# One 512-column product for both halves of the activations in the 256-token dense tiles

## Chip, core and metric

The kernel runs on one core of one Trainium2 chip. The metric is device time in microseconds for one launch: 3149.86 us is the median of three runs before the change (3148.79 to 3150.08). The engines are named as the profile names them: PE (TensorE matmul), PEld (TensorE weight load), DVE (VectorE), ACT (ScalarE), POOL (GpSimd) and SP (SyncE, which issues most DMAs).

## What is computed

Two model blocks in float32 on 256 tokens of width 2048: a gated recurrent mixer, an attention layer with shared keys and values, then a block of convolution and windowed attention, and a layer that looks up experts by product keys and uses all 16384 expert rows. What matters here are the dense products with 2048 rows. In the second block, for example:

```python
proj = xn @ w_in + b_in                       # 256 x 2048 by 2048 x 3328
x = x + mixed @ w_out
qh = (xt @ peer_w_q).reshape(T, PEER_HEADS, 2, PEER_HALF)
...
v1, i1 = lax.top_k(sub[:, :, 0], PEER_TOPK)   # top 16 of 128, per token, head and half
```

The first block's dense products cover 272 positions (16 fixed ones and the 256 tokens) or the 256 tokens alone.

## The kernel before

Every dense product is done with split operands. A weight tile of 128 x 128 is split by `split` (lines 191 to 193): ACT copies it to a rounded type (`wh`, line 192) and DVE subtracts to get the rest (`wl`, line 193). The activations are split the same way into a high and a low part, which lie side by side in one tile `x[128, 2, 16, 272]` (`new_xs`, line 205). A product is then three matmuls per block of 128 rows: wh by high, wl by high, wh by low, all into one accumulator of 128 x 256 or 128 x 272 (`Dense.products`, line 117, matmul at line 127). A job with 16 blocks has 48 such matmuls. PSUM holds two accumulators (`psacc`, two buffers), each in a bank of its own.

Jobs run in a list, in the order in which they are appended, under `run`. At the start of job n, `run` calls the read-out (`evac`) of job n-1, then issues the four quarters of job n's products. Ahead of the first quarter it issues the split of the second half of job n+1's weights, and ahead of the third the split of the first half of job n+2's. `wh` and `wl` have two buffers per half, so a split waits until the matmuls of two tiles before have read the buffer. After each quarter `run_side` issues a piece of side work (attention, convolution, top-16 searches) until a credit per job is used up (`BUDGET`). The order of all queues is thus fixed when the program is built, and each engine works through its queue in that order.

The stages that hold jobs of 256 tokens and 16 blocks, with the read-out of each, are:

- stage f (587 to 1036 us): attention projections. 32 of its 64 tiles have 256 columns (query and gate); DVE scales the accumulator into `pj` (line 763).
- f-out (1036 to 1132 us): 16 tiles; DVE adds the accumulator to `hT` (line 899).
- stage b (1132 to 1376 us): 26 tiles of the second block's input product; DVE scales into `qb` (lines 1416, 1518) or `gt` (line 1524). For the 10 tiles of line 1416 ACT then adds a bias.
- stage p (1498 to 1605 us): 16 tiles of `peer_w_q`; ACT alone copies the accumulator into `qh` (line 1891). The side work is `peer_head` and `peer_pairs`: for each head the top 16 of 128 on DVE (`top16`, lines 1731 to 1741) and the top 16 of the candidates.

Behind p comes a stretch (1605 to about 1860 us) in which the first 29 `UBlock` jobs multiply expert rows (line 1967) while the rest of the top-16 work and then the building of gate grids (`grid_gen`, lines 1998 to 2021) run beside them; the hook of the 30th block waits until the grids are issued in full (`v_hook`). From block 29 on, a `UBlock` already uses the other form of product: one matmul of wh with both activation halves, 512 columns (line 1958), and one of wl with the high half, 256 columns (line 1959), and a read-out in which ACT copies the second half (line 1977), DVE adds the first (line 1978), and ACT applies the activation function (line 1979). The rest, to 3148 us, alternates such blocks with `VPair` jobs (line 2111).

Of the kernel before, what the change touches and what calls it, by code (L numbers as in the profile page):

```python
# [8 lines left out]
F32 = mybir.dt.float32  # L9
# [6 lines left out]
AF = mybir.ActivationFunctionType  # L16
OP = mybir.AluOpType
# [4 lines left out]
KB = 16  # L22
NM = 16
S = 256
# [56 lines left out]
class Dense:  # L81
# [4 lines left out]
    def __init__(self, k, chunk, j, xs, ts, evac, hook=None, after=None):  # L86
        self.k, self.chunk, self.j, self.xs, self.ts = k, chunk, j, xs, ts
        self.evac_fn, self.hook, self.after = evac, hook, after
        self.w = [None, None]

    def load(self):
        while len(self.chunk.setdefault("raws", [])) * 8 < self.chunk["nk"]:
            self.load_part()
# [23 lines left out]
    def products(self, b0, b1, by_block=True):  # L117
        k, c = self.k, self.chunk
        xh, xl = self.xs()
        n = c["nk"] // 2  # L120
        blocks = [(b, t) for b in range(b0, b1) for t in range(3)]
        if not by_block:
            blocks.sort(key=lambda bt: (0, 2, 1)[bt[1]])
        for b, t in blocks:
            wh, wl = self.w[b // n]
            a, x = ((wh, xh), (wl, xh), (wh, xl))[t]
            k.PE.matmul(self.acc, a[:, b % n], x[:, c["k0"] + b, self.ts], start=(b == 0 and t == 0),  # L127
                        stop=(b == c["nk"] - 1 and t == 2))

    def open(self):  # L130
        self.acc = self.k.psacc.tile([128, self.ts.stop - self.ts.start], F32, name="acc")

    def mm(self):
        self.open()
# [1 line left out]
        return [lambda i=i: self.products(i * nk // 4, (i + 1) * nk // 4) for i in range(4)]  # L136

    def evac(self):
        self.evac_fn(self.acc)


class Kit:
# [3 lines left out]
def body(tc, x, meta, gamma_lb, a_norm, a_w_in, a_out_norm, a_w_out, kv_norm, kv_w, fox_b_f,  # L146
         fox_k_norm, b_norm, b_w_in, b_q_norm, b_w_out, positions, norm1_g, w_in, b_in, conv_w,
         conv_b, ln_g, ln_b, q_norm_g, k_norm_g, sinks, w_out, norm2_g, peer_w_q, sub_keys,
         peer_u, peer_v, cst, out, dbg=None):
    with tc.manual_schedule():  # L150
        _body(tc, x, meta, gamma_lb, a_norm, a_w_in, a_out_norm, a_w_out, kv_norm, kv_w, fox_b_f,
              fox_k_norm, b_norm, b_w_in, b_q_norm, b_w_out, positions, norm1_g, w_in, b_in, conv_w,
              conv_b, ln_g, ln_b, q_norm_g, k_norm_g, sinks, w_out, norm2_g, peer_w_q, sub_keys,
              peer_u, peer_v, cst, out, dbg)


def _body(tc, x, meta, gamma_lb, a_norm, a_w_in, a_out_norm, a_w_out, kv_norm, kv_w, fox_b_f,
# [4 lines left out]
    V, A, G, PE = nc.vector, nc.scalar, nc.gpsimd, nc.tensor  # L162
    K = Kit()
# [10 lines left out]
    early = tc.alloc_tile_pool(name="early", bufs=1)  # L174
    psacc = tc.alloc_tile_pool(name="psacc", bufs=2, space=PSUM, reuse_waits="tile")
    ps = tc.alloc_tile_pool(name="psA", bufs=1, space=PSUM, reuse_waits="tile")
    wk = tc.alloc_tile_pool(name="wkA", bufs=1, reuse_waits="tile")
# [18 lines left out]
    def split_g(h_blk, g, oh, ol):  # L196
        A.activation(oh, h_blk, AF.Copy, scale=g)
        V.scalar_tensor_tensor(ol, h_blk, g, oh.bitcast(F32), op0=OP.mult, op1=OP.subtract)

    def flat(t):  # L200
        return t.rearrange("p h t -> p (h t)")

    whole = {}

    def new_xs(pool, tag):
        x = pool.tile([128, 2, KB, T], F32R, name=tag)
        whole[tag] = x
        return x[:, 0], x[:, 1]

    def wview(w):  # L210
        return w.rearrange("(k p) c -> p k c", p=128)
# [13 lines left out]
    def rsqrt_steps(pool, ps_list, scale, out_t, tags, less=None):  # L225
        n = sum(math.prod(p.shape[1:]) for p in ps_list)
        v, r, t = (pool.tile([128, n], F32, name=g) for g in tags)
        srcs, c = [], 0
        for p in ps_list:
            m = math.prod(p.shape[1:])  # L230
            srcs.append((slice(c, c + m), p if len(p.shape) == 2 else flat(p)))
            c += m

        for c, src in srcs:
            V.tensor_scalar(v[:, c], src, scale, EPS, op0=OP.mult, op1=OP.add)
        if less is not None:
            V.tensor_tensor(v, v, less, op=OP.subtract)
        yield 0.1 + n / 960
        yield 1
        A.activation(r, v, AF.Ln)  # L240
        A.activation(r, r, AF.Exp, scale=-0.5)
        A.activation(t, r, AF.Square)
        yield 3
        V.scalar_tensor_tensor(t, t, -0.5, v, op0=OP.mult, op1=OP.mult)
        out_t = r if out_t is None else out_t
        V.scalar_tensor_tensor(out_t, t, 1.5, r, op0=OP.add, op1=OP.mult)
        yield 0.2 + n / 480
        return out_t
# [217 lines left out]
    for t in vtz:  # L466
        G.memset(t[:, 0], 0.0)

    xh, xl = new_xs(xs1, "xs")
    cur = {"x": (xh, xl)}  # L470
    tok = ((0, NM), (NM, 128), (NM + 128, 128))
    st = {}
# [24 lines left out]
    def start_sums(g):  # L497
        for i in (1, 2):
            n = tok[i][1]
            sq = wk.tile([128, 2, T], F32, name="sq", bufs=2)  # L500
            src = x_raw[i][:, g * 512:(g + 1) * 512]
            if i == 2:
                V.scalar_tensor_tensor(flat(sq)[:n, :512], src, 1.0, src, op0=OP.mult, op1=OP.mult,
                                       accum_out=ssp[:n, i, g:g + 1])
            else:
                A.activation(flat(sq)[:n, :512], src, AF.Square, accum_out=ssp[:n, i, g:g + 1])
            if g == 3:
                V.tensor_reduce(ss[:n, i:i + 1], ssp[:n, i], axis=AX.X, op=OP.add)
# [14 lines left out]
    def start_rest():  # L523
        p = ps.tile([128, 4, 128], F32, name="tp", bufs=3)
        PE.transpose(p[:, 0], pk2, ident)
        for i in range(2):
            PE.transpose(p[:, 1 + i, :124], pk3[:, i], ident[:124, :124])
        PE.transpose(p[:, 3], pk1, ident)
        V.tensor_copy(par[:, 128:], p[:, 0])
        V.tensor_copy(par[:, 16:128], p[:, 3, 16:])  # L530
        V.tensor_copy(taps.rearrange("p (a b) -> p a b", a=2), p[:, 1:3, :124])
        gm = wk.tile([128, KB], F32)
        g0 = par[:, P1["gamma"]:P1["gamma"] + KB]
        g1 = par[:, P1["gamma"] + KB:P1["gamma"] + 2 * KB]
        V.tensor_tensor(gm, g0, g1, op=OP.max)
        ge = wk.tile([128, 2, KB], F32)
        V.tensor_tensor(ge[:, 0], g0, gm, op=OP.subtract)
        V.tensor_tensor(ge[:, 1], g1, gm, op=OP.subtract)
        A.activation(ge, ge, AF.Exp)
        V.tensor_tensor(gm, ge[:, 0], ge[:, 1], op=OP.add)  # L540
        V.reciprocal(gm, gm)
        V.tensor_tensor(lbs[:, 0], ge[:, 0], gm, op=OP.mult)
        V.tensor_scalar(lbs[:, 1], lbs[:, 0], -0.5, 0.5, op0=OP.mult, op1=OP.add)
        V.tensor_tensor(lbs[:, 0], lbs[:, 0], lbs[:, 1], op=OP.add)
        st["o"] = new_xs(early, "ys")
# [205 lines left out]
    def chunk(wv, c0, k0=0, nk=KB):  # L751
        return {"wv": wv, "c0": c0, "k0": k0, "nk": nk}
# [157 lines left out]
    def a_out_hook():  # L910
        st["kv"] = new_xs(xs1, "xs")
# [279 lines left out]
    for i, (hp, u) in enumerate(order):  # L1191
        wv, c0, xs, ts, half, bufs = fspec[u]
# [335 lines left out]
    for t in "q0 c0 q1 c1 q2 c2 q3 c3".split():  # L1528
        n = int(t[1])
# [118 lines left out]
    for i, part in enumerate(PARTS):  # L1648
# [3 lines left out]
        k0, nk = (0, 8) if part == "c" else (8 + 2 * int(part[0]), 2 * len(part))  # L1652
        for c2 in range(KB // 2):
            c = chunk(wvo, c2 * 256, k0, nk)
            for j in range(2):
                jobs.append(Dense(K, c, j, lambda: st["mix"], xcols,
                                  lambda acc, n=c2 * 2 + j, f=on_tile: f(n, acc), hook if c2 + j == 0 else None))
# [225 lines left out]
    for h in range(8):  # L1883
        c = chunk(wvq, h * 256)
# [316 lines left out]
```

## Time and profile before

| | |
|---|---|
| runs before | 3149.86 us median, 3148.79 to 3150.08 |
| profiled execution | 3149.75 us, span 3147.9 us |
| mean granted TensorE clock | 0.992 |
| PE busy | 3068.7 us (97% of the span), 20863 matmuls |
| DVE busy | 2394.4 us (76%) |
| ACT busy | 1657.4 us (53%) |

The profiled execution lies 0.11 us under the median and 1.85 us over its own span. Shares of busy time are means over stages with different limits, so they are read stage by stage: the view of windows gives each engine's busy time in a stretch, the view of waits says who waited for whom, and the timeline gives the start of single instructions. The duration of a matmul in the profile covers its way through the array and overlaps the next; the pace is the distance from start to start.

### The profile page before, as it was taken

The numbers are of one execution on the slowest core, as the hardware profiler recorded it, in microseconds if no ns is written. First come the engines' busy times: TensorE is split into PE (matmuls) and PEld (weight loads), VectorE is DVE, ScalarE is ACT, GpSimd is POOL, SyncE is SP. The second block draws the span as 40 slices with busy tenths as digits, with TensorE's granted clock in tenths as the row PEclk, the third lists the DMA queues.
The fourth block names the chain that finished last, engine by engine and source line by source line (L and its number), as shares of the span: only waits on it lengthen the run. The fifth ranks groups of instructions, "written<-read, shape, count | busy, mean of one in ns | idle before, by whom it ended". The sixth has DMA issues, their size and how long they took to land.

```text
span 3147.9 us, 51907 instructions
## 1 busy us (share of the span) xinstructions
PE 3068.7 (97%) x20863; PEld 2834.8 (90%) x20863; DVE 2394.4 (76%) x3828; ACT 1657.4 (53%) x2640; POOL 250.9 (8%) x185
## 2 busy tenths in 40 slices
PE   8999999999999999988999989999999999999999
PEld 7999999999999999988998987888888888888887
DVE  6666666665666667768788988888888898989874
ACT  5455554566566556746543445544545454545443
POOL 1000000000000000000000003211112020303020
PEclk9999999999999999998999999999999999999999
DMA  6545445554544553324533777777777676767754
GB/s 208 155 138 157 138 134 161 160 157 140 161 148 148 173 172 111 109 89 140 183 136 123 211 219 204 202 205 205 204 196 210 189 220 185 214 189 226 196 192 161
DMA packets 362130, 540.64 MB, mean 172 GB/s; under 512 B 13771, under 2 KB 270128, under 8 KB 356112
## 3 DMA queue, kind: packets, MB, share of 16 engines
q1 hardware_dynamic: 325248, 501.33, 54.1%
q10 hardware_dynamic: 33200, 16.85, 1.9%
q0 software_dynamic: 3440, 19.13, 1.8%
q8 instruction: 164, 2.69, 0.4%
q14 instruction: 78, 0.64, 0.1%
HBM read 518.38 MB, written 18.87 MB: 171 GB/s over the span
## 4 chain that ended last, share of the span: by engine, by line
PE 85%; DVE 10%; ACT 3%; issue 1%; POOL 1%; DMA 1%; SPq 0%; DVEq 0%; ACTq 0%
PE acc L127 37%; PE y L2111 22%; PE acc L1958 11%; PE acc L1959 6%; DVE wl L193 3%; PE cv L1475 1%; DVE o L2001 1%; ACT wh L192 1%; PE acc L1967 1%; DVE o L1999 1%; DVE tb L2000 1%; DVE tb L1998 1%; PE o L1110 1%; DVE e L1814 0%; DVE qh L1932 0%
## 5 line engine op out<-in xcount | busy, mean ns | idle before, releaser
L193 DVE TENSOR_TENSOR wl<-raw,wh 128x1024 fp32r<-128x1024 f32 (+1 forms) x724 | 863.1, 1199 | 513.5 <-ACT wh L192 511.3
L192 ACT ACTIVATE wh<-raw 128x1024 fp32r<-128x1024 f32 (+1 forms) x724 | 728.8, 1016 | 466.1 <-PE acc L127 324.9
L127 PE MATMUL acc<-xs,wh 128*128 128x272 f32 (+1 forms) x4064 | 794.6, 292 | 21.1 <-ACT xs L192 11.4
L127 PEld LDWEIGHTS acc<-xs,wh 128*128 128x128 f32 x4064 | 648.0, 191 | 25.4 <-ACT xs L192 12.5
L127 PE MATMUL acc<-xs,wl 128*128 128x272 f32 (+1 forms) x2032 | 584.9, 288 | 0.0
L127 PE MATMUL acc<-ys,wh 128*128 128x256 f32 (+1 forms) x2880 | 555.2, 288 | 5.4 <-DVE qb L1416 3.1
L1958 PE MATMUL acc<-xs,wh 128*128 128x512 f32 x1584 | 556.3, 393 | 0.0
L127 PEld LDWEIGHTS acc<-ys,wh 128*128 128x128 f32 x2880 | 454.6, 189 | 9.2 <-ACT sinT L1255 3.3
L192 ACT ACTIVATE wh<-qh 128x512 fp32r<-128x512 f32 x396 | 250.7, 633 | 388.3 <-DVE qh L1932 359.4
L1959 PE MATMUL acc<-xs,wl 128*128 128x256 f32 x1584 | 443.8, 280 | 0.8 <-DVE wl L193 0.8
L127 PE MATMUL acc<-ys,wl 128*128 128x256 f32 (+1 forms) x1440 | 406.6, 282 | 0.0
L1932 DVE STREAM_TRANSPOSE qh<-raw 128x512 f32<-128x512 f32 x396 | 403.5, 1058 | 1.7 <-DMA raw<-in_peer_u_dram 1.7
L127 PEld LDWEIGHTS acc<-xs,wl 128*128 128x128 f32 x2032 | 386.8, 191 | 0.9
L1958 PEld LDWEIGHTS acc<-xs,wh 128*128 128x128 f32 x1584 | 297.6, 188 | 67.2
L2111 PE MATMUL y<-wh,ah 128*128 128x512 f32 x1024 | 317.9, 391 | 2.4 <-ACT wh L192 2.4
L2111 PE MATMUL y<-wl,ah 128*128 128x512 f32 x1024 | 317.1, 391 | 1.5 <-DVE wl L193 1.5
L2111 PE MATMUL y<-wh,al 128*128 128x512 f32 x1024 | 316.7, 390 | 0.0
L193 DVE TENSOR_TENSOR wl<-qh,wh 128x512 fp32r<-128x512 f32 x396 | 296.2, 756 | 19.3
L1959 PEld LDWEIGHTS acc<-xs,wl 128*128 128x128 f32 x1584 | 297.8, 188 | 5.0 <-DVE wl L193 1.6
L127 PEld LDWEIGHTS acc<-ys,wl 128*128 128x128 f32 x1440 | 272.5, 189 | 1.7
L2111 PEld LDWEIGHTS y<-wl,ah 128*128 128x128 f32 x1024 | 192.3, 188 | 43.3 <-DVE wl L193 2.3
L2111 PEld LDWEIGHTS y<-wh,al 128*128 128x128 f32 x1024 | 192.5, 188 | 42.0
(473 smaller groups left out, 3555.8 us busy)
## 6 DMA issues: line engine op xcount, KB each, us to landing
raw<-in_peer_v_dram SPq DMA_DIRECT2D x128, 1024.0 KB, 5.2
raw<-in_peer_u_dram SPq DMA_DIRECT2D x396, 256.0 KB, 5.1
raw<-in_a_w_in_dram SPq DMA_DIRECT2D x64, 1024.0 KB, 5.9
raw<-in_kv_w_dram SPq DMA_DIRECT2D x32, 1024.0 KB, 5.6
raw<-in_b_w_in_dram SPq DMA_DIRECT2D x32, 1024.0 KB, 5.3
raw<-in_peer_u_dram SPq DMA_DIRECT2D x29, 1024.0 KB, 4.9
raw<-in_w_in_dram SPq DMA_DIRECT2D x26, 1024.0 KB, 5.3
raw<-in_a_w_out_dram SPq DMA_DIRECT2D x16, 1024.0 KB, 5.4
```

The lines of the kernel that those rows point to most:

```text
L127: k.PE.matmul(self.acc, a[:, b % n], x[:, c["k0"] + b, self.ts], start=(b == 0 and t == 0), stop=(b == c["nk"] - 1 and t == 2))
L192: A.activation(dh, src, AF.Copy)
L193: V.tensor_tensor(dl, src, dh.bitcast(F32), op=OP.subtract)
L1110: PE.matmul(po[:, b * 128:(b + 1) * 128], vt[:, i], pts[:, 2 * b + i], start=(i == 0), stop=(i == nt - 1))
L1475: PE.matmul(acc, dgs[k0][:, k - k0], hp[:, k:k + S], start=(k == 0), stop=(k == n - 1))
L1932: V.transpose(ut[g].rearrange("p k (e s) -> p e k s", e=4), u[:, :, k:k + 4])
L1958: PE.matmul(self.acc, uh[:, k % 8], both[:, :, k, xcols], start=(k == 0), stop=False)
L1959: PE.matmul(self.acc[:, 0], ul[:, k % 8], nh[:, k, xcols], start=False, stop=(k == KB - 1))
L1967: PE.matmul(self.acc, a[:, k % 8], c[:, k, xcols], start=(k == 0 and t == 0), stop=(k == KB - 1 and t == 2))
L1998: V.tensor_tensor(e2, words, at(wd[:, 1], t0), op=OP.is_equal)
L1999: V.tensor_tensor(o2, e2, at(one, t0), op=OP.mult)
L2111: PE.matmul(self.y[tb][q], a[:, r, ts], c[:, q * 512:q * 512 + 512], start=(self.place == 0 and h == 0 and i == 0), stop=(self.place == GR ...
```

## The change

A job is wide if it has 16 blocks and 256 columns. Its accumulator becomes 128 x 2 x 256. For each block it issues one matmul of wh with both halves of the activations (512 columns) and one of wl with the high half (256 columns, into the first half of the accumulator). At the read-out `meet` is called first: ACT copies the second half of the accumulator to a tile in SBUF, DVE adds the first half in place, and the job's own read-out gets that tile instead of the accumulator. The tile is `hsq` (one buffer, shared with the sums of squares) up to the end of f-out, and `mt` (one buffer) in stages b and p. 90 tiles are wide: 32 in f, 16 in f-out, 26 in b, 16 in p. The tiles of 272 columns, the 32 tiles of 8 blocks between b and p, and the expert blocks are as before.

```diff
+        self.wide = chunk["nk"] == KB and ts.stop - ts.start == S
...
     def products(self, b0, b1, by_block=True):
         k, c = self.k, self.chunk
         xh, xl = self.xs()
         n = c["nk"] // 2
+        if self.wide:
+            both = k.whole[id(xh)]
+            for b in range(b0, b1):
+                wh, wl = self.w[b // n]
+                k.PE.matmul(self.acc, wh[:, b % n], both[:, :, c["k0"] + b, self.ts], start=(b == 0), stop=False)
+                k.PE.matmul(self.acc[:, 0], wl[:, b % n], xh[:, c["k0"] + b, self.ts], start=False, stop=(b == c["nk"] - 1))
+            return
...
     def open(self):
-        self.acc = self.k.psacc.tile([128, self.ts.stop - self.ts.start], F32, name="acc")
+        n = self.ts.stop - self.ts.start
+        self.acc = self.k.psacc.tile([128, 2, n] if self.wide else [128, n], F32, name="acc")
...
     def evac(self):
-        self.evac_fn(self.acc)
+        self.evac_fn(self.k.meet(self.acc) if self.wide else self.acc)
...
+    def meet(acc):
+
+        t = (wk if "hpad" in st else early).tile([128, S], F32, name="mt" if "hpad" in st else "hsq")
+        A.activation(t, acc[:, 1], AF.Copy)
+        V.tensor_tensor(t, t, acc[:, 0], op=OP.add)
+        return t
```

In the changed kernel lines from the middle of the file on stand 20 further down (line 193 is 202 there, line 1891 is 1911).

The first place is ACT's queue in stage p, at the end of one tile; before:

```order
L1891 ACTIVATE qh<-acc 128x256
L192 ACTIVATE wh_16760<-raw_16476 128x1024
L192 ACTIVATE wh_16794<-raw_16654 128x1024
L1755 ACTIVATE skT<-tp 128x256
L1891 ACTIVATE qh<-acc 128x256
L192 ACTIVATE wh_16844<-raw_16656 128x1024
```

and now:

```order
L212 ACTIVATE mt<-acc 128x256
L1911 ACTIVATE qh<-mt 128x256
L201 ACTIVATE wh_15720<-raw_15472 128x1024
L201 ACTIVATE wh_15746<-raw_15624 128x1024
L1775 ACTIVATE skT<-tp 128x256
L212 ACTIVATE mt<-acc 128x256
L1911 ACTIVATE qh<-mt 128x256
```

ACT's copy into `qh` now stands behind a first copy into `mt`, and reads a tile that DVE has to finish in between; the split of the next weights (`wh`) is still behind it.

The second place is DVE's queue in the same stage (L1731 to L1741 and, shifted, L1751 to L1761 are the top-16 search); before:

```order
L1731 MAX v_16219<-tb 128x8 x2
L1733 MAX_INDEX i_16924<-v_16219,tb 128x8 x2
L1736 MATCH_REPLACE tb<-v_16219,tb 128x128 x2
L1738 MAX v_16219<-tb 128x8 x2
L193 TENSOR_TENSOR wl_17016<-raw_16831,wh_17015 128x1024
L1741 MAX_INDEX i_16924<-v_16219,tb 128x8 x2
```

and now:

```order
L1751 MAX v_15257<-tb 128x8 x2
L1753 MAX_INDEX i_15855<-v_15257,tb 128x8 x2
L1756 MATCH_REPLACE tb<-v_15257,tb 128x128 x2
L1758 MAX v_15257<-tb 128x8 x2
L213 TENSOR_TENSOR mt<-mt,acc 128x256
L202 TENSOR_TENSOR wl_15937<-raw_15775,wh_15936 128x1024
L1761 MAX_INDEX i_15855<-v_15257,tb 128x8 x2
```

The new addition (`mt<-mt,acc`) stands straight ahead of the subtraction that makes `wl`, and behind the top-16 work of the tile before. Nothing else changes its place.

## Rows read from the trace of the kernel before

**Rows 1.** The page: busy time of each engine, and the chain that ended last, by engine.
```profile
PE 3068.7 (97%) x20863; PEld 2834.8 (90%) x20863; DVE 2394.4 (76%) x3828; ACT 1657.4 (53%) x2640; POOL 250.9 (8%) x185
...
PE 85%; DVE 10%; ACT 3%; issue 1%; POOL 1%; DMA 1%; SPq 0%; DVEq 0%; ACTq 0%
```

**Rows 2.** Windows by stage; columns: stretch, its length, busy us (instructions), PEclk, DMA, GB/s.
```profile
core 0: us, PE busy (x) PEld busy (x) DVE busy (x) ACT busy (x) POOL busy (x), PEclk, DMA share, GB/s
587.40:1036.00 448.60, 445.85 (x3565) 437.26 (x3563) 293.57 (x526) 276.16 (x437) 0.00 (x0) 1.00 0.50 151
1036.00:1131.80 95.80, 93.77 (x781) 93.57 (x779) 58.91 (x85) 46.75 (x70) 1.58 (x4) 0.98 0.56 176
1131.80:1376.40 244.60, 229.70 (x1691) 219.03 (x1690) 159.56 (x293) 152.58 (x325) 0.00 (x0) 0.97 0.36 113
...
1527.00:1605.20 78.20, 78.20 (x670) 78.20 (x669) 68.95 (x270) 38.48 (x64) 4.33 (x6) 1.00 0.54 172
1605.20:1732.00 126.80, 119.63 (x993) 116.76 (x993) 113.99 (x397) 52.69 (x97) 0.00 (x0) 1.00 0.35 125
1732.00:1859.00 127.00, 113.23 (x1190) 109.20 (x1190) 122.75 (x169) 61.27 (x116) 0.00 (x0) 1.00 0.73 216
```

**Rows 3.** Windows: eleven whole tiles of f-out (48 matmuls each), same columns.
```profile
1063.69:1126.17 62.48, 62.48 (x530) 62.48 (x529) 39.65 (x55) 31.11 (x44) 0.00 (x0) 1.00 0.61 194
```

**Rows 4.** Timeline of PE: one expert block, 32 matmuls, first and next job's first.
```profile
2007.13 0.40 PE L1958 MATMUL acc<-xs,wh 128*128 128x512 f32 x1
2007.36 0.28 PE L1959 MATMUL acc<-xs,wl 128*128 128x256 f32 x1
...
2012.70 0.40 PE L2111 MATMUL y<-wh,ah 128*128 128x512 f32 x1
```

**Rows 5.** ACT's read-outs by source line: ns least/median/most, first and last start.
```profile
L1891 ACT ACTIVATE qh<-acc x16: 367/386/388, 1507.7 to 1605.2; 128x256 f32<-128x256 f32 x16
...
L1977 ACT ACTIVATE ga<-acc x99: 357/384/387, 1892.3 to 3023.8; 128x256 f32<-128x256 f32 x99
```
**Rows 6.** The same for the addition in the expert blocks, and who waited for it.
```profile
L1978 DVE TENSOR_TENSOR ga<-ga,acc x99: 406/420/423, 1892.8 to 3024.3; 128x256 f32<-128x256 f32 x99
...
  ACT ga L1979: 78.5, 99
```

**Rows 7.** Timeline of PE: where f-out waits for a free accumulator; idle time in brackets.
```profile
1050.70 0.48 PE L127 MATMUL acc<-xs,wh 128*128 128x256 f32 x1 [2.03 <-DVE hT L899]
```

**Rows 8.** Timeline of ACT in stage p, over two tile ends.
```profile
1558.97 0.39 ACT L1891 ACTIVATE qh<-acc 128x256 f32<-128x256 f32 x1 [0.95 <-PE acc L127]
1559.25 1.05 ACT L192 ACTIVATE wh<-raw 128x1024 fp32r<-128x1024 f32 x1
1561.81 1.06 ACT L192 ACTIVATE wh<-raw 128x1024 fp32r<-128x1024 f32 x1 [1.50 <-PE acc L127]
1565.53 0.38 ACT L1891 ACTIVATE qh<-acc 128x256 f32<-128x256 f32 x1 [2.66 <-PE acc L127]
```

**Rows 9.** Timeline of DVE in the same stretch.
```profile
1557.05 1.21 DVE L193 TENSOR_TENSOR wl<-raw,wh 128x1024 fp32r<-128x1024 f32 x1
...
1559.61 0.48 DVE L1738 MAX8 v<-tb 128x8 f32<-128x128 f32 x2
1560.34 1.23 DVE L193 TENSOR_TENSOR wl<-raw,wh 128x1024 fp32r<-128x1024 f32 x1 [0.26 <-ACT wh L192]
```

**Rows 10.** Waits of DVE from 1527 to 1605.2 us: total us, times, longest.
```profile
DVE wl L193 <- ACT wh L192: 8.5, 13, 1.5
```

**Rows 11.** Timeline of DVE after stage p, three waits around the gates.
```profile
1713.36 0.69 DVE L193 TENSOR_TENSOR wl<-tp,wh 128x512 fp32r<-128x512 f32 x1 [1.49 <-ACT wh L192]
1716.79 0.69 DVE L193 TENSOR_TENSOR wl<-tp,wh 128x512 fp32r<-128x512 f32 x1 [0.47 <-ACT wh L192]
1718.73 0.69 DVE L193 TENSOR_TENSOR wl<-tp,wh 128x512 fp32r<-128x512 f32 x1 [1.25 <-ACT wh L192]
```

**Rows 12.** Waits of PE from 1732 to 1859 us.
```profile
PE g L2019 <- DVE o L2001: 13.6, 12, 2.8
```

More of the change, by code (lines that the diff above doesn't have):

```diff
@@ L198, in split_g @@
         V.scalar_tensor_tensor(ol, h_blk, g, oh.bitcast(F32), op0=OP.mult, op1=OP.subtract)
+    def meet(acc):
[3 more added lines that the diff above has]
+        return t
+    K.meet = meet
     def flat(t):
         return t.rearrange("p h t -> p (h t)")
-    whole = {}
+    K.whole = whole = {}
+    keep = []
     def new_xs(pool, tag):
         x = pool.tile([128, 2, KB, T], F32R, name=tag)
-        whole[tag] = x
-        return x[:, 0], x[:, 1]
+        h = x[:, 0]
+        whole[tag] = whole[id(h)] = x
+        keep.append(h)
+        return h, x[:, 1]
     def wview(w):
```

## The prediction

> **What bounds the kernel now.** I read the page first: PE is busy for 97% of the span, and 85% of the chain that ended last is PE's [rows 1]. So what PE no longer has to stream counts, unless another engine is the limit where it is saved. The view of windows by stage tells where that is so [rows 2]. In f and f-out PE is busy for all but 2.8 of 448.6 us and 2.0 of 95.8 us, while DVE and ACT are below two thirds. In b PE has 15 us without work, DVE and ACT are at 65% and 62%. In p it is another picture: PE is busy without a gap, but DVE is busy for 68.95 of 78.2 us, so it has only 9.25 us left, and 8.5 of these are spent waiting for `wh` [rows 10]. Behind p, from 1605 to 1859 us, DVE sets the pace: 122.75 of the last 127 us, and there it is PE that waits, 12 times, 13.6 us, for the operands `o` that DVE builds [rows 2, 12]. The reader should keep this in mind: p lies directly ahead of a stretch that runs at DVE's speed, and its DVE work is in the same queue.
>
> **What the change removes on PE.** The pace of the narrow form is read from eleven tiles of f-out without other work between them: 62.48 us, 5.680 us a tile, 118.3 ns a matmul [rows 3]. The wide form already runs in the expert blocks: the same 16 blocks, from the first matmul to the next job's first, 2007.13 to 2012.70, take 5.57 us [rows 4]. So a product of 512 columns costs nearly what two of 256 cost (0.23 and 0.12 us from start to start), and a wide tile saves only 0.11 us, 2%, although it has a third fewer matmuls. For 74 tiles in f, f-out and b that is 8.1 us; with the 16 of p 9.9 us. The granted clock is 1.00 in both rows, so no difference of clock is in this. Bounds: 0.09 to 0.12 us a tile, by the last digit of the timeline.
>
> The Trainium skill (TensorE: Matmul & The Clock Gate, section "Back-to-back issue gap") puts the distance of warm matmuls at N / 2.4 + 2.5 ns. By that a narrow tile would take 5.24 us and a wide one 5.20, and the 74 tiles would save 3.0 us instead of 8.1. The rows show 118.3 ns, not 109, so I keep to the rows.
>
> **What it adds at the read-out.** ACT's copy of the second half: 0.38 us; DVE's addition: 0.42 us [rows 5, 6]. Both exist in this trace in the same form, so these prices are not in doubt. What they cost is a matter of what stands behind them in each queue.
>
> In f, f-out and in the 16 gate and value tiles of b, ACT goes from its copy straight to the split of the next weights. DVE's addition and its own read-out (0.42 each) lie beside that `wh` copy of 1.05 us, for which DVE's next `wl` had to wait anyway. In the 10 tiles of b with a bias ACT already waited for DVE; there the chain gets 0.8 us longer. All of it is covered by two thirds use of both engines and by two accumulators, of which each has a whole tile (5.7 us) to come free. I take 0; if that cover were gone, each read-out would cost up to 0.8 us. One place has no cover: in f-out the third tile waits 2.03 us for an accumulator that a DVE addition frees [rows 7]; it now also waits for the copy, +0.4 us.
>
> **Stage p is different.** Here ACT's copy into `qh` reads what DVE has added, and the copy that makes `wh` is queued behind it; on DVE the addition stands directly ahead of the `wl` that needs this `wh`. So at each tile end DVE adds (0.42), ACT copies to `qh` (0.28 until its next instruction starts), ACT makes `wh` (1.06), and DVE has nothing else to do until then; with two hand-overs of 0.04 that is 1.8 us from the start of the addition to the start of `wl` [rows 6, 8, 9]. Before, DVE came from its top-16 search and found `wh` ready or nearly so: 0.26 us of waiting at 1560.34 [rows 9]. 12 of the 16 read-outs fall between 1527 and 1605.2 us. They add 12 x 1.8 = 21.6 us to DVE's queue; DVE's former idle time, 9.25 us, goes into that. The first three, where DVE has room, and the last one I put at 1.3 us together. DVE then ends stage p 13.6 us later than it would have.
>
> PE does not feel this at once. The `wl` made at 1560.34 to 1561.57 is needed only in the second half of the following tile, about 1565.53 + 2.84 = 1568.4, so there are 6.8 us of slack [rows 8, 9]. Beyond that PE waits for `wl`, its 1.8 us saved in p are gone, and DVE enters the next stretch late.
>
> **What is made up behind p.** From 1732 to 1859 us nothing can be: DVE has 4.25 us idle in 127, and PE waits for it [rows 2, 12]. From 1605 to 1732 us DVE is idle for 12.8 us. A wait behind `wh` is only saved if ACT waited for PE there, and most of these follow DVE's own results through ACT; I take the three around the gates, 1.49 + 0.47 + 1.25 = 3.2 us [rows 11]. The bounds are 0 and 12.8. After 1859 us PE is the limit again and everything is shifted as a whole.
>
> **The sum**, against the profiled execution of 3149.75 us: -8.1 (74 tiles) + 0.4 (f-out) + 13.6 (DVE's delay in p) - 3.2 (made up) = +2.7, so 3152.5 us. With the bounds of what is made up, 3142.9 to 3155.7. The median of the runs before is 0.11 us higher than this execution, which changes nothing. A measurement of this kernel can tell about 0.2%, 6.3 us, from no change.
>
> **Rivals.**
>
> 1. *DVE absorbs the read-outs of p.* 12 additions of 0.42 us are 5.0 us, less than the 9.25 idle, and PE has 6.8 us of slack at each tile. If the hand-over to ACT costs DVE no idle time, or the whole delay is made up before 1732 us, all 90 tiles save 0.11 us: 3149.75 - 9.9 + 0.4 = 3140.3 us. For it: PE waits for nothing in p now. Against it: the order of both queues, and 78.5 us in 99 cases, 0.79 us each, that ACT waits for the same addition in the expert blocks [rows 6].
>
> 2. *Slower: read-outs in b and f come free too late.* The accumulator is now freed by a DVE addition that waits for an ACT copy, and this copy stands behind ACT's side work (the exponentials and scalings of the attention heads). If ACT is more than a tile less 0.8 us, 4.9 us, behind PE, PE waits for one of its two accumulators. With about 10 read-outs exposed at 0.8 us, 8 us come on top of the forecast: 3160.5 us. For it: ACT is at 62% in f and in b and works in bursts. Against it: PE waits in f for 2.8 us in all, and b's tiles leave more time than 5.7 us because other matmuls lie between them.
>
> 3. *The wide product saves nothing in these stages*, since side matmuls break up the tiles; then -8.1 falls away and the time is 3149.75 + 0.4 + 13.6 - 3.2 = 3160.6 us. Against it: the pace of rows 3 and 4 is that of the plain stream, and most of a tile is that. The formula of the skill quoted above would lie between this and my forecast.
>
> **How the numbers follow.** Forecast 0.52, rival 1 0.24, rival 2 0.19, rival 3 0.05. The forecast and its bounds lie within 6.3 us of no change, rival 1 is faster by more, rivals 2 and 3 are slower by more: faster 0.24, same 0.52, slower 0.24. The forecast's own range is 3142.9 to 3155.7; to leave out no more than 2 in 10 the range has to reach to the rivals on both sides, 3140 to 3161 us. This is a change whose gain is real but small, and it is spent in the one stage in which DVE has no time to spare.
>
> **What would show it.** Right: `wl` in p waiting for `wh` for 1.4 us at nearly every tile, DVE without other idle time there, PE with waits for `wl` from the middle of p on, stage f-out shorter by some 1.3 us, and the start of p earlier by about 7.7 us but 1859 us reached 2 to 3 us later than before. Wrong: PE without waits in p and the end of p earlier by 9 us (rival 1); waits of PE for `hsq` or `mt` in f or b (rival 2); tiles of f-out still at 5.68 us (rival 3).

## The result and the profile after

The changed kernel is slower: 3166.89 us median (3163.53 to 3169.66, 6 runs) against 3149.32 us (3146.83 to 3150.41, 6 runs) in the same session. The ratio is 1.0055, with a 95% interval of 1.0045 to 1.0065. That is 17.6 us more, outside the predicted range, which ended at 3161. The profiled execution took 3166.95 us with a span of 3165.2, so it is close to the median.

The page of the changed kernel, the same two lines as [rows 1]:

```profile
PE 3068.9 (97%) x19423; PEld 2768.6 (87%) x19423; DVE 2430.6 (77%) x3918; ACT 1681.2 (53%) x2730; POOL 251.4 (8%) x185
...
PE 80%; DVE 13%; ACT 4%; issue 2%; POOL 1%; DMA 1%; SPq 0%; DVEq 0%; ACTq 0%
```

PE has 1440 matmuls fewer and is busy just as long. The share of PE in the chain that ended last has gone from 85% to 80%, and DVE's from 10% to 13%. ACT and DVE each have 90 instructions more: the read-outs of 90 tiles, 32 in f, 16 in f-out, 26 in b and 16 in p.

The view of windows shows where the time went. Each stretch runs from the first matmul of a stage to the first of the next: f, f-out, b, p, and the first 29 expert blocks behind p. The columns are those of [rows 2].

```profile
589.00:1037.40 448.40, 444.53 (x3053) 413.08 (x3051) 305.71 (x556) 283.75 (x469) 0.00 (x0) 1.00 0.52 151
1037.40:1130.10 92.70, 90.79 (x524) 79.52 (x523) 66.14 (x101) 52.34 (x86) 1.57 (x4) 1.00 0.58 182
1130.10:1378.90 248.80, 229.81 (x1273) 200.14 (x1272) 170.91 (x320) 160.07 (x352) 0.00 (x0) 0.96 0.36 110
1501.00:1621.20 120.20, 110.96 (x673) 97.49 (x671) 90.82 (x312) 61.63 (x113) 5.05 (x7) 0.99 0.46 150
1621.20:1899.70 278.50, 256.13 (x2367) 249.09 (x2366) 249.66 (x580) 122.98 (x229) 3.21 (x3) 0.99 0.57 175
```

The kernel before, the last two of these stretches:

```profile
1498.40:1606.80 108.40, 108.40 (x929) 108.30 (x927) 87.06 (x299) 59.55 (x100) 5.06 (x7) 1.00 0.53 166
1606.80:1883.10 276.30, 255.37 (x2367) 248.46 (x2367) 248.97 (x577) 122.00 (x227) 2.76 (x3) 0.99 0.57 176
```

Stage p went from 108.4 to 120.2 us and is the bulk. Stage b went from 244.6 to 248.8, although its PE work should have shrunk. f gained 0.2 us, and f-out 3.1, of which about half is the granted clock (0.98 before in [rows 2], 1.00 now). Behind p, 2.2 us more were lost, and nothing was made up.

In p the trace shows the predicted chain. DVE after, around two tile ends (start, duration, engine, line, operation; idle time in brackets):

```profile
1562.13 0.40 DVE L213 TENSOR_TENSOR mt<-mt,acc 128x256 f32<-128x256 f32 x1
1563.96 1.23 DVE L202 TENSOR_TENSOR wl<-raw,wh 128x1024 fp32r<-128x1024 f32 x1 [1.43 <-ACT wh L201]
...
1569.50 0.40 DVE L213 TENSOR_TENSOR mt<-mt,acc 128x256 f32<-128x256 f32 x1
1571.33 1.23 DVE L202 TENSOR_TENSOR wl<-raw,wh 128x1024 fp32r<-128x1024 f32 x1 [1.43 <-ACT wh L201]
```

ACT in the same stretch:

```profile
1562.57 0.42 ACT L1911 ACTIVATE qh<-mt 128x256 f32<-128x256 f32 x1 [3.33 <-DVE mt L213]
1562.89 1.99 ACT L201 ACTIVATE wh<-raw 128x1024 fp32r<-128x1024 f32 x2
1564.78 0.36 ACT L1775 ACTIVATE skT<-tp 128x256 f32<-128x256 f32 x1
1565.05 0.37 ACT L212 ACTIVATE mt<-acc 128x256 f32<-128x256 f32 x1
1569.93 0.42 ACT L1911 ACTIVATE qh<-mt 128x256 f32<-128x256 f32 x1 [4.51 <-DVE mt L213]
```

ACT copies the second half at 1565.05 and then stands still for 4.51 us, because its next instruction needs DVE's addition, and DVE gets to that addition only at 1569.50, behind another `wl` and its top-16 search. Only then can ACT make `wh`. So DVE in its turn waits 1.43 us. From the start of the addition to the start of `wl` it is 1.83 us both times. The view of waits for the whole of p:

```profile
ACT qh L1911 <- DVE mt L213: 49.3, 15, 5.1
DVE wl L202 <- ACT wh L201: 23.5, 19, 1.4
...
PE g L1780 <- ACT skT L1775: 3.4, 2, 3.2
PE acc L126 <- DVE mt L213: 3.0, 3, 1.6
```

### The profile page after: what moved, and what is told of

Same layout as the page of the kernel before. It is cut to its first block, busy times and chain, and to the rows that moved or that the text cites. A ratio compares the mean times of both kernels' runs of the same rounds, so it can differ in the third digit from the quotient of the medians.

```text
span 3165.2 us, 49162 instructions
## 1 busy us (share of the span) xinstructions
PE 3068.9 (97%) x19423; PEld 2768.6 (87%) x19423; DVE 2430.6 (77%) x3918; ACT 1681.2 (53%) x2730; POOL 251.4 (8%) x185
## 4 chain that ended last, share of the span: by engine, by line
PE 80%; DVE 13%; ACT 4%; issue 2%; POOL 1%; DMA 1%; SPq 0%; DVEq 0%; ACTq 0%
PE acc L135 22%; PE y L2131 22%; PE acc L1978 11%; PE acc L126 7%; PE acc L1979 6%; DVE wl L202 4%; PE acc L127 4%; ACT wh L201 2%; PE cv L1495 1%; DVE o L2021 1%; PE acc L1987 1%; DVE o L2019 1%; DVE tb L2020 1%; DVE tb L2018 1%; PE o L1130 0%
## 5 line engine op out<-in xcount | busy, mean ns | idle before, releaser
L135 PE MATMUL acc<-xs,wh 128*128 128x272 f32 (+1 forms) x3552 | 701.2, 294 | 19.3 <-ACT xs L201 11.4
L135 PEld LDWEIGHTS acc<-xs,wh 128*128 128x128 f32 x3552 | 567.3, 190 | 23.8 <-ACT xs L201 12.5
L135 PE MATMUL acc<-xs,wl 128*128 128x272 f32 (+1 forms) x1776 | 511.6, 289 | 0.0
L126 PE MATMUL acc<-ys,wh 128*128 128x512 f32 x1184 | 439.6, 410 | 7.0 <-DVE mt L213 7.0
L1978 PEld LDWEIGHTS acc<-xs,wh 128*128 128x128 f32 x1584 | 297.4, 188 | 67.1
L135 PEld LDWEIGHTS acc<-xs,wl 128*128 128x128 f32 x1776 | 337.6, 190 | 0.9
L127 PE MATMUL acc<-ys,wl 128*128 128x256 f32 x1184 | 333.7, 282 | 0.0
L1979 PEld LDWEIGHTS acc<-xs,wl 128*128 128x128 f32 x1584 | 297.6, 188 | 4.8 <-DVE wl L202 1.4
L126 PEld LDWEIGHTS acc<-ys,wh 128*128 128x128 f32 x1184 | 224.7, 190 | 57.2 <-DVE mt L213 8.6
L127 PEld LDWEIGHTS acc<-ys,wl 128*128 128x128 f32 x1184 | 224.7, 190 | 1.7
```

What stands on the lines that cost most here:

```text
L126: k.PE.matmul(self.acc, wh[:, b % n], both[:, :, c["k0"] + b, self.ts], start=(b == 0), stop=False)
L127: k.PE.matmul(self.acc[:, 0], wl[:, b % n], xh[:, c["k0"] + b, self.ts], start=False, stop=(b == c["nk"] - 1))
L1978: PE.matmul(self.acc, uh[:, k % 8], both[:, :, k, xcols], start=(k == 0), stop=False)
L1979: PE.matmul(self.acc[:, 0], ul[:, k % 8], nh[:, k, xcols], start=False, stop=(k == KB - 1))
```

## The experiments

Twelve kernels ran. The expectations of x1 to x4 misname or miscount tiles: f, f-out, b and p have 32, 16, 26 and 16 wide ones, all of p's are query tiles, and x4 has all 90 wide, which by the prediction's price saves 9.9 us and not 8.1. The theories are decided by what single stages lost; the times of x1, x2, x7, x8 and x14 lie 0.1 to 0.5 us outside the ranges expected for the theory that held. The table shows what each stage lost or gained against the profiled execution of before, in us, by the starts of the same matmuls in the trace. "Half clock" is the change of the time that the trace's clock record has PE at 1.2 GHz instead of 2.4, over a to p and the stretch behind; 3.4 us of it are worth about 1.7 us where PE sets the pace. In p of the change PE no longer does: the change and x2 lose the same 11.7 us there, with 3.4 and 6.8 us more at half clock. Stage a runs the same code in all.

| run | a | f | f-out | b | p | behind p | half clock |
|---|---|---|---|---|---|---|---|
| the change | +1.6 | -0.2 | -3.1 | +4.3 | +11.7 | +2.2 | +10.2: a, b, p, behind +3.4 each, f-out -3.4 |
| x1, p narrow | -0.3 | -0.2 | -1.5 | +1.9 | 0.0 | -0.1 | 0 |
| x2, p alone | +1.9 | 0.0 | 0.0 | +0.1 | +11.7 | +2.1 | +13.6: a +3.4, p +6.8, behind +3.4 |
| x3, p in place | +1.0 | -0.2 | -1.5 | +4.4 | -1.2 | +1.2 | +10.2: a, b, behind +3.4 each |
| x4, products alone | +1.3 | -2.0 | -3.0 | -4.0 | -1.2 | +0.9 | 0: a, behind +3.4, f-out, b -3.4 |
| x5, read-out alone | +2.0 | +1.4 | -1.5 | +3.7 | +12.0 | +1.6 | +10.2: f-out -3.4, b +3.4, p +6.8, behind +3.4 |

**Run x1_p_narrow.** Only p goes back to narrow products: each stage sets its name, and `WIDE` lists f, f-out and b.

```diff
-        self.wide = chunk["nk"] == KB and ts.stop - ts.start == S
+        self.wide = chunk["nk"] == KB and ts.stop - ts.start == S and k.stage in WIDE
...
+    K.stage = "p"
```

> The wide product stays in the 42 + 11 tiles of f and f-out and in the tiles of b; the 12 q and kv tiles of p and everything behind them are as before. Theory A (most of the lost time is p's two-step read-out, where DVE's add stands behind DVE's wait for the next weights' low part, and what p shifts behind it): the 11.7 us that p lost and the 2.6 us lost behind it go away, the stretch from p's start to the up-projections' first tile is within 1 us of before, and the time is 3152 to 3154 us, that is 3 to 4 us above before, all of it from b. Rival B (the loss is spread over all tiles, PE loses by what breaks them and by stretches at half clock): more than half of the 17.6 us stays, 3158 us or more.

Measured: 3151.9 us against 3150.26, ratio 1.0010 (1.0000 to 1.0019). The 11.7 us and what followed behind p are gone: theory A. Of stage b's loss of 4.3 us, 1.9 stay.

**Run x2_p_alone.** The same edit, and `WIDE` lists p alone.

> Only the 12 tiles of p behind the 256-token boundary use the wide product; f, f-out and b are as before. Theory A: p loses 11 to 13 us by itself and the time is 3161 to 3164 us. Rival B (p loses only because it begins in another phase, after what b lost, or by a stretch at half clock that b's shift moved into it): p alone loses under 6 us and the time is below 3156 us.

Measured: 3164.51 us, ratio 1.0043 (1.0027 to 1.0060). p alone loses 11.7 us, as much as in the whole change. Theory A again; nothing ahead of p is needed.

**Run x3_p_in_place.** What ACT and DVE do in p's read-out, without ACT's step that waits for DVE:

```diff
-                A.activation(st["qh", h][:, j], acc, AF.Copy)
+                q = st["qh", h][:, j]
+                A.activation(q, acc[:, 1], AF.Copy)
+                V.tensor_tensor(q, q, acc[:, 0], op=OP.add)
```

> All tiles wide as in the change, but in p ACT copies the accumulator's second half straight into the q or kv tile and DVE adds the first half in place; ACT's third step, which waited 47.3 us in all for DVE's add, is gone, and one ACT read of 256 columns a tile less. Theory A1 (p's delay is ACT standing behind DVE: ACT waits for the add, then casts the next weights late, DVE waits 1.4 us for them, and its add comes late again): DVE's waits for the next weights' high part fall from 16.7 us to under 4 us, p loses under 3 us, and the time is 3153 to 3156 us. Rival A2 (the delay is DVE's extra busy time, 12 adds of 0.42 us in a stretch that DVE bounds, or PE's wait for the accumulator that only DVE can release): p still loses 6 us or more and the time is 3159 us or more.

Measured: 3152.99 us, ratio 1.0008 (0.9998 to 1.0017). p is now 1.2 us shorter than before the change, exactly what the products alone gain there. The number of DVE's additions is the same. One figure missed: DVE's waits for `wh` over the whole of p fell from 23.5 to 8.7 us, where under 4 was expected. Before the change they came to 16.9 us (8.5 of them in the middle of p [rows 10]), and PE waited for nothing in p.

**Runs x13_p_second_copy and x14_p_copy_on_dve.** x3 takes away a wait and also 16 copies on ACT. These two separate them. x13 adds to x3 a copy on ACT that waits for nothing and that nobody reads; x14 is the change itself with the copy of the sum on DVE.

```diff
 # x13, on top of x3
+                A.activation(wk.tile([128, S], F32, name="mt"), acc[:, 1], AF.Copy)
 # x14, on top of the change
-                A.activation(st["qh", h][:, j], acc, AF.Copy)
+                V.tensor_copy(st["qh", h][:, j], acc)
```

> As the run with p read out in place, and ACT copies the accumulator's second half once more into a tile that nobody reads: ACT has as many copies a tile as in the change, but none of them waits for DVE. Theory A1 (p lost its 11.7 us by ACT's third step waiting for DVE's add): p stays within 1.5 us of the in-place run (1.2 us shorter than before the change) and the time is 3151 to 3155 us. Rival A3 (p lost because ACT has another copy of 0.38 us a tile ahead of the next weights): p loses 4 us or more against the in-place run and the time is 3157 us or more.

> The change as it is, but in p the copy of the sum into the query tile runs on DVE, behind DVE's add, where it ran on ACT, which waited for it. Theory A1: ACT no longer waits for the add, so p loses under 3 us although DVE does still more (about 0.2 to 0.4 us more in each of 16 tiles): 3153 to 3157 us. Rival A2 (DVE's own work is what p lacks): p loses what it did or more, 3165 us or more.

Measured: 3152.2 us, ratio 1.0012 (1.0003 to 1.0022), and 3152.63 us, ratio 1.0013 (1.0003 to 1.0023). Stage p in x3, by the view of windows:

```profile
1502.20:1609.40 107.20, 107.20 (x673) 96.05 (x671) 91.60 (x314) 59.28 (x99) 5.06 (x7) 1.00 0.51 168
```

In x13:

```profile
1502.10:1609.30 107.20, 107.20 (x673) 96.09 (x671) 91.29 (x314) 63.33 (x115) 5.05 (x7) 1.00 0.52 168
```

In x14:

```profile
1504.20:1611.40 107.20, 107.20 (x673) 96.06 (x671) 95.27 (x330) 59.07 (x98) 5.06 (x7) 1.00 0.52 168
```

All three take 107.2 us with PE busy throughout, against 120.2 in the change. In x13 ACT works more than in the change (63.33 us against 61.63), in x14 DVE does (95.27 against 90.82). Neither costs anything. So it is not the work of either engine that p lacked but ACT's wait for DVE: theory A1 is shown, A2 and A3 fall.

**Runs x4_products_alone and x5_readout_alone** split the change in two.

```diff
 # x4
-        self.evac_fn(self.k.meet(self.acc) if self.wide else self.acc)
+        self.evac_fn(self.acc[:, 0] if self.wide else self.acc)
 # x5: narrow products and accumulators, and in meet()
-        A.activation(t, acc[:, 1], AF.Copy)
-        V.tensor_tensor(t, t, acc[:, 0], op=OP.add)
+        A.activation(t, acc, AF.Copy, scale=0.0)
+        V.tensor_tensor(t, t, acc, op=OP.add)
```

> All 74 tiles use the wide product, but the read-out takes only the accumulator's first half, as the narrow one did: no added copy, no added add. What is left out is the second half, the product of the weights' high part with the activations' low part. So this is the PE side of the change alone. By the prediction's own term the time falls by 8.1 us, to 3141 us. By the traces' shift of single tiles (0.09 us in the tiles that nothing breaks, 0.02 to 0.08 where other matmuls stand between) it falls by 3 to 5 us, to 3144 to 3146 us. If PE itself loses by the wide form where DVE bounds p, or by half-clock stretches, it is 3149 us or more.

> All products narrow as before the change, but each of the 90 tiles (32 of f, 16 of f-out, 26 of b, 16 of p) is read out in two steps as in the change: ACT copies the accumulator times zero, DVE adds the accumulator to it; so the read-out's cost alone. If product and read-out simply add, it is before + 17.6 + 8.8 (what the products alone gained) = about 26 us more than before, 3175 to 3179 us, of it 13 us in p, 6 to 9 us in b and about 2 us in f. If the read-out hurts only because the wide form lets PE run ahead of it (less cover per tile), the read-out alone costs less than the whole change did: below 3167 us.

Measured: products alone 3140.45 us, ratio 0.9973 (0.9961 to 0.9984), so 9.8 us faster. The read-out alone 3168.31 us, ratio 1.0057 (1.0041 to 1.0072), so 18.7 us slower. PE's side of the change is a gain, then. That it comes so close to the 9.9 us that the prediction's price gives for 90 tiles is luck: f, f-out, b and p together are 10.3 us shorter, but about 3.4 of that is 6.8 us less at half clock, so the products save about 6.9. The parts do not add, as -9.8 + 18.7 is not 17.6, and the read-out alone is not much dearer or cheaper than the whole change: neither guess of x5 held. The table says why. In p the products give 1.2 us and the read-out takes 12.0, but both together lose 11.7, not 10.8: while ACT and DVE set the pace, what PE saves there is lost. In b it is the same. Only in f and f-out do both halves roughly add, in f-out apart from the clock.

**Run x7_b_alone.** Only b wide.

> Only b's 26 tiles are wide, with the read-out of the change. Theory A (b's read-outs come late where PE waits for them: the next tile behind kv1, the rotary product behind c0a1): the stretch from b's start to the packed weights' products is 2 to 4.5 us longer than before and the time 3152 to 3155 us. Rival B (b lost only because f and f-out handed over 1.7 us earlier, so that waits filled up that anyway stood there): b alone is within 1 us of before, 3149 to 3151 us.

Measured: 3155.47 us (3149.64 to 3156.79, 10 runs), ratio 1.0014 (1.0005 to 1.0024). b lost 4.3 us without any help from f and f-out: theory A. About 1.7 us of it is 3.4 us more at half clock, and the profiled execution is the slowest of the ten. In x1 the same tiles lost only 1.9. Most of the difference lies in one tile, the second value tile of the convolution's first pair, in which PE waits for the rotary product's input. Its window in x1:

```profile
1164.50:1174.60 10.10, 7.81 (x44) 6.59 (x43) 7.81 (x12) 4.75 (x7) 0.00 (x0) 1.00 0.68 211
```

The same tile in x7:

```profile
1168.41:1180.14 11.73, 9.38 (x45) 7.88 (x44) 7.82 (x12) 4.76 (x7) 0.00 (x0) 0.85 0.62 183
```

PE is idle for 2.3 us in x1 and 2.4 us in x7. In x7 a stretch at half clock follows (mean 0.85), and the tile takes 1.6 us longer. It is so in the change, too.

**Runs x8_fo_p_in_place and x11_conv_p_in_place.** x8 is x3 with b narrow; x11 makes b's 16 convolution tiles wide again.

> f, f-out and p wide, b narrow, p read out in place (as in the run with p in place). Theory A: f -0.2, f-out -1.7, b 0, p -1.1: the time is 3146.5 to 3148 us, 2 to 3.5 us below before. Rival B (b's waits fill up whatever time f and f-out hand over, or half-clock stretches take it): 3149 us or more.

> As the run before it, and of b the 16 tiles of the convolution's gates wide too, its 10 tiles of keys, values and queries narrow. Theory A (b's loss hangs on the read-outs that attention's chain waits for: kv1 and the queries): b loses less than half of its 4.3 us, and the conv tiles may give 1 to 1.5 us back: 3145.5 to 3149 us. Rival B (any read-out in b delays DVE, where the rotary step stands in a row with the others): b loses 2 us or more, 3149.5 to 3152 us.

Measured: x8 3146.34 us, ratio 0.9991 (0.9982 to 1.0000); x11 3147.43 us, ratio 0.9992 (0.9983 to 1.0001). Stage b is 1.8 us shorter than before in x8 and 1.9 in x11, each with 3.4 us less at half clock. So the 16 tiles cost nothing and gain nothing, and b's loss needs the 10 tiles with a bias to be wide.

**Runs x15_b_bias_on_dve and x16_b_narrow_bias_on_dve.** In these 10 tiles ACT adds the bias to what DVE has made; it waited 21.8 us for DVE in b of x3. Before the change it already waited 22.2 us there; what has grown is PE's waits behind it, from 14.8 us in all of b to 19.1 in the change. The edit takes that wait away, on top of x3 (all wide) and of x8 (b narrow):

```diff
-                A.activation(qb[:, j], qb[:, j], AF.Identity, bias=pcol("b_in", base + j))
+                V.tensor_scalar(qb[:, j], qb[:, j], pcol("b_in", base + j), None, op0=OP.add)
```

> All tiles wide, p in place, and in b the bias of the keys, values and queries is added by DVE right behind its product, where ACT waited for DVE to add it (21.8 us in all in the change). Theory A (b's loss has p's cause, ACT standing behind DVE): b, 4.4 us longer in the run with p in place, is at most 1 us longer than before, and the time is 3146 to 3150 us. Rival B (b's loss is the path itself: rotary product and normalization wait for a read-out that has one more DVE step): b stays 2 us or more longer than before, 3150.5 us or more.

> The control: f, f-out and p wide with p in place, b narrow, and b's bias on DVE. If the moved bias does nothing by itself, the time is that of the run with b narrow, 3145.5 to 3148 us; if ACT's wait cost b something already before the change, it is 1 us or more below that. Against the run before it, the difference is what b's wide tiles give or take once ACT doesn't wait in b: by theory A they gain 0.5 to 2.5 us, by rival B they lose 2 us or more.

Measured: x15 3146.15 us, ratio 0.9990 (0.9981 to 0.9999); x16 3144.25 us, ratio 0.9981 (0.9972 to 0.9991). Stage b in x3, by the view of windows:

```profile
1131.10:1380.00 248.90, 229.98 (x1273) 200.29 (x1272) 170.96 (x320) 160.14 (x352) 0.00 (x0) 0.96 0.35 110
```

In x15:

```profile
1130.70:1372.80 242.10, 226.44 (x1275) 197.96 (x1273) 173.92 (x330) 156.69 (x342) 0.00 (x0) 0.96 0.36 113
```

In x16:

```profile
1131.20:1371.60 240.40, 226.62 (x1691) 216.63 (x1689) 163.19 (x304) 149.21 (x316) 0.00 (x0) 0.97 0.37 115
```

With wide tiles b goes from 248.9 to 242.1 us by one instruction that changes its engine (1.7 us of it the clock, 3.4 us less at half speed), so theory A of x15 holds. That ACT's wait cost b something even before the change shows against x8: 242.8 us there, with the same time at half clock, 240.4 here. So part of x15's gain would come without wide tiles too. What the wide tiles themselves cost is the difference between wide and narrow: with the bias on ACT 6.2 us (x3 against x8, 3.4 of it the clock), with the bias on DVE 1.6 us (x15 against x16, 1.7 of it the clock). The second comparison fits neither theory's figure for x16: apart from the clock the wide tiles then give and take nothing. The loss of b that is not the clock, 2.8 us, hangs on ACT's bias step behind DVE, then. Whether it is the step's wait or its work on ACT (0.5 us a tile) no run separates in b; x13 did that for p alone.

x16 beats both kernels: 3144.25 us, 0.19% below the kernel before and some 22 us below the change (in another session). Its interval excludes no change by 0.09%.

## Why the prediction was wrong

The sum said +2.7 us; in the profiled execution the last matmul starts 17.0 us later than before. Of the 14.3 us between them, b makes 7.2, what was to be made up behind p 5.4 and f 3.3; p and f-out came out 1.9 and 1.7 us better than forecast, and stage a and the rest of the program add 2.0. The start of p was to come 7.7 us earlier and came 2.6 us later. By the terms of the sum:

- **Stage p, 13.6 us of delay: right in mechanism, nearly in size.** Wait for wait it went as written: 1.43 us ahead of `wl`, 1.83 us from addition to `wl` where 1.8 was forecast. DVE's first split of [rows 11] ran at 1713.36 us and now runs at 1728.78, 15.4 us later, and p had begun 2.6 us late: p delayed DVE by 12.8 us. PE lost 11.7 of them in p and 1.1 right behind it, where its wait for `wl` was this before:

```profile
1617.44 0.72 PE L1942 MATMUL tp<-cs,raw 128*128 128x128 f32 x4 [0.40 <-DVE wl L193]
```

  and is this now:

```profile
1632.92 0.72 PE L1962 MATMUL tp<-cs,raw 128*128 128x128 f32 x4 [1.49 <-DVE wl L202]
```

  A detail was off: inside p PE stood less for `wl` (1.3 us) than for the accumulator that the late addition frees (3.0 us) and for ACT's `skT` behind it (3.4 and 1.0 us). And rows 2 made me explain the delay by DVE having only 9.25 us free. x14 lets DVE work 4.5 us more than the change does, and p loses nothing. It was the order, not the room.
- **"In the 10 tiles of b with a bias ACT already waited for DVE; there the chain gets 0.8 us longer ... I take 0": this step failed.** Forecast for b: 26 x -0.11 = -2.9 us; measured: +4.3, an error of 7.2 us and half of the whole, of which about 1.7 is the clock. It is the chain that I had costed tile by tile in p, with a bias in the place of the copy, and I had ruled it free by the mean use of the two engines and by the time that an accumulator has to come free. The timeline of ACT after the change, in b:

```profile
1164.58 0.51 ACT L1437 ACTIVATE qb<-qb,par 128x256 f32<-128x256 f32 x1 [1.81 <-DVE qb L1436]
1164.99 1.99 ACT L201 ACTIVATE wh<-raw 128x1024 fp32r<-128x1024 f32 x2
```

DVE there:

```profile
1166.07 1.23 DVE L202 TENSOR_TENSOR wl<-raw,wh 128x1024 fp32r<-128x1024 f32 x1 [1.53 <-ACT wh L201]
...
1168.12 0.48 DVE L1303 SCALAR_TENSOR_TENSOR qb<-qb,par,r 128x256 f32<-128x256 f32 x1
```

And PE:

```profile
1168.66 1.14 PE L1317 MATMUL lgb<-qb,cs 128*128 128x256 f32 x4 [2.40 <-DVE qb L1303]
```

  ACT waits for DVE, makes `wh` late, DVE waits for `wh`, and the normalization that PE needs is queued behind that `wl`. Before, PE waited there for 0.52 us:

```profile
1167.79 1.13 PE L1297 MATMUL lgb<-qb,cs 128*128 128x256 f32 x4 [0.52 <-DVE qb L1283]
```

  Without ACT's bias step (x15) this wait of PE's is gone from the list, and so is the convolution's wait for ACT (2.1 us in the change, 1.2 before). What stays is the accumulator behind the keys, 4.1 us where it was 3.1, and the rotary product of the queries waits for the normalization 2.8 us in all where it was 1.2. In all PE waits 15.7 us in b of x15, 0.9 more than before.
- **The saving on PE, 0.11 us a tile: right in kind, a fifth too large.** Eleven tiles of f-out, the same as in [rows 3]:

```profile
1063.10:1124.55 61.45, 61.45 (x354) 53.91 (x353) 44.31 (x66) 35.33 (x55) 0.00 (x0) 1.00 0.62 195
```

  5.586 us a tile instead of 5.680, so 0.09 us: the lower bound. In x4 f gained 2.0 us, where 32 x 0.11 = 3.5 was forecast. In five of the seven wide tiles of f that no side matmul breaks up the trace of x4 shows the full 0.09 us; the 25 others save 0.055 in the mean, so rival 3 holds in part. f-out gained 1.5 us apart from the clock (x1), which is 16 x 0.09 alone. It is near the forecast 1.8 - 0.4 by luck, as the 0.4 did not come: the third tile waits 1.91 us for its accumulator, where it was 2.03 [rows 7], since ACT's copy (at 1050.08 us) runs beside a `wl` (from 1050.21) that DVE makes ahead of its addition (1051.35). An estimate from the Trainium skill's formula for the gap of an isolated matmul (TensorE: Matmul & The Clock Gate, "Back-to-back issue gap") made the saving 0.04 us a tile; the trace, at 0.09, does not agree with it.
- **The read-outs in f, taken at 0: wrong by 1.4 to 1.8 us.** x5 puts them at 1.4; with the wide products f kept 0.2 of 2.0 us. Against x4, 0.8 of these 1.8 us are lost at one place, where ACT squares what DVE's read-out has made and PE needs the squares. ACT after the change:

```profile
736.85 0.63 ACT L1021 ACTIVATE sq<-pj 128x512 f32<-128x512 f32 x1 [2.88 <-DVE pj L783]
```

  and PE, which waits for nothing there in x4:

```profile
737.54 1.13 PE L1033 MATMUL tp<-sq,ones 128*128 128x256 f32 x4 [0.69 <-ACT sq L1021]
```

  This and b are rival 2 in part: its place was right, and its cause, ACT behind PE by its own work, was not; at the places shown ACT was behind DVE.
- **3.2 us made up behind p: wrong, nothing was made up.** The three waits around the gates, which were to shrink because DVE comes late, stand as in [rows 11], each 15.4 us later:

```profile
1728.78 0.69 DVE L202 TENSOR_TENSOR wl<-tp,wh 128x512 fp32r<-128x512 f32 x1 [1.49 <-ACT wh L201]
...
1732.20 0.69 DVE L202 TENSOR_TENSOR wl<-tp,wh 128x512 fp32r<-128x512 f32 x1 [0.47 <-ACT wh L201]
1734.15 0.69 DVE L202 TENSOR_TENSOR wl<-tp,wh 128x512 fp32r<-128x512 f32 x1 [1.26 <-ACT wh L201]
```

  ACT's work was late by as much as DVE's. Of the 2.2 us lost behind p instead, 1.1 are p's delay, as said above. The other 1.1 come later in the stretch. x3, x13 and x14, with nothing to make up, lose 0.7 to 0.9 us there too, each like the change with 3.4 us more at half clock.
- **The granted clock, which the sum left out.** Stage a, which the change does not touch, lost 1.6 us and had one more stretch at half clock; but x5 lost 2.0 us there without one, so the clock alone does not explain it. f-out won about 1.6 by one stretch less. Such differences come and go between executions and were no part of any step.

## What to carry to other kernels

Ask of each added read-out step not how busy its engines are but whether an instruction of one engine now waits for a late instruction of the other, and what is queued behind the waiting one. Here DVE's half of a weight split waits for ACT's, and a read-out that goes ACT, DVE, ACT makes each wait for the other, tile after tile: 0.4 us of addition cost 0.8 us a tile. In p, ending the read-out on DVE (in place, or with the last step moved there) took the whole loss away, in x14 although DVE did more work.

## What the hardware showed beyond that

- After some waits of about 2 us PE's granted clock falls from 2.4 to 1.2 GHz for 3.4 us, and after others just as long it does not. At the second value tile above PE waits 2.29 us both in x1 and in x3; x1 keeps its clock, x3 falls to half. In f-out PE waits 1.91 us both in x1 and in the change; there x1 falls and the change does not. A fall costs about 1.7 us where PE sets the pace, so such a wait can cost nearly twice its length. x7's ten times lie in two groups, three from 3149.6 to 3151.3 us and seven from 3155.1 to 3156.8. That the clock alone parts them is not shown; only one of them has a trace.
- DVE working for 95.27 of 107.2 us (x14) delayed nothing. In the change it worked for 90.82 of 120.2 us, and its late additions held up ACT and PE.
